# Weight splits through three buffers of 1024 columns instead of two of 1152

## The chip, the core and the metric

The kernel runs on one core of a Trainium2 chip. The metric is the device time of one execution in microseconds (us), and the median over several runs stands for a kernel. The engines have short names here: PE multiplies matrices (PEld is its loading of weights), DVE, ACT and POOL work element by element, SP only issues DMAs. Every engine works off its own queue in order.

## What is computed

A two-layer encoder on one sequence of 512 positions with 1024 channels. Each layer is a half-weighted FFN, four mixers side by side on slices of one input projection, and a second half-weighted FFN.

```python
D_MODEL, SEQ, DEPTH, D_FF = 1024, 512, 2, 2816
N_GROUPS = GROUP_HEADS = 4          # GROUP_WIDTH 256, HEAD_DIM 64

def swiglu(x, w_gate, w_up, w_down):
    return (jax.nn.silu(x @ w_gate) * (x @ w_up)) @ w_down
...
# per layer: x += 0.5 * ffn1(norm(x)); x += mixers(norm(x)) @ w_out; x += 0.5 * ffn2(norm(x))

# rwkv7_mixer: a state per head, forward and backward over the sequence
def step(S, inp):
    r_t, k_t, v_t, kk_t, a_t, w_t = inp
    sa = jnp.einsum('bhvk,bhk->bhv', S, -kk_t)
    S = (S * w_t[:, :, None, :] + sa[..., None] * (kk_t * a_t)[:, :, None, :]
         + v_t[..., None] * k_t[:, :, None, :])
    return S, jnp.einsum('bhvk,bhk->bhv', S, r_t)
...
# retention_mixer: scores with a decay, states before and after a chunk, a norm per head, a gate
# mla_mixer: latent queries and keys (ranks 384 and 128), softmax attention over all 512 positions
# short_conv_mixer: three taps, two gates
```

## The kernel before

All activations lie transposed, 128 channels on the partitions by 512 positions: `x[d]` for d in 0 to 7. A matmul in full precision is made of three in a fast format: `split` (L320) turns a raw weight tile into a rounded part `w_hi`, cast on ACT at L327, and a rest `w_lo`, subtracted on DVE at L328; `mm3` then issues hi·hi (L338), hi·lo (L339) and lo·hi (L340). Both parts come from rings of two buffers of 1152 columns of fp32. Raw weights come by DMA from SP into a ring of two buffers of 2048 columns (`load`).

The FFN (L344) goes over 11 of the 22 blocks of hidden channels at a time: a load of 2048 columns, split into 1024 for the gate (tile `pg`) and 1024 for the up projection (`pu`), 24 matmuls each; then eight output tiles `pd`, whose weights come in splits of 768 and 640 columns.

The mixers (`Mixers.run`) use `proj` for 128 columns of the input projection (tile `pj`, a split of 1024, done in pieces of 512), and `proj_nat` for two projections with positions on the partitions (tile `pn`, L502 to L504): `wrv` with 256 columns, the RWKV values, and `wtv` with 288, the retention's values and MLA's rotary key. `proj_nat` holds all weights of a projection at once, as two halves of four channel blocks each: 1024 columns for `wrv`, 1152 for `wtv`. `gd` and `ckv` are the weights projected after `wrv`, `tg` (two blocks, the retention's gate) those after `wtv`.

The RWKV state runs in eight chain steps. In each, on PE: scores `psG` L1059, values into `zy` L1078 and L1081, eight solves with the inverted blocks `NR` (L1090), the state (L1105) and eight outputs (L1123). Between them DVE and ACT copy: `Zs`, the solved values `ch` (DVE L1093 for one direction, ACT L1094 for the other), `Sd` and `Yn`. Beside the chain PE has matmuls of MLA (`m_pq`, the scores `m_sc` L781, the transposes of probabilities `m_ptp` L793) and of retention (`ret_ps`, `ret_po`, `ret_ss`, the broadcasts `ret_pb`). A softmax tile takes on DVE a maximum L783, a scaling of it L784, a reciprocal L787 and the scaling of the tile `m_p` L788, with an exponential on ACT (L786) between. Retention ends (`retention_end`) with a reciprocal root in many short steps (L235 to L241), copies `ret_sq` L253, products `ret_o` L671 and a split `ys` L513; the RWKV output is normed in L1155 to L1164. Then comes the output projection `po`.

The order in each queue is set when the program is built: a scheduler plays the instructions on a timeline of its own and takes, of those that are ready and whose buffers are free, the earliest in the code. Splits are moved ahead by 4000 places (`AHEAD`), and `in_turn` fixes the order within a group. So buffer counts set the order of instructions.

Tiles of the mixers and FFNs come from two pools: `vt`, NV = 19 tiles of 128x1024, and `ft`, NFS = 23 tiles of half that size.

Of the kernel before, what the change touches and what calls it, by code (L numbers as in the profile page):

```python
# [8 lines left out]
F32 = mybir.dt.float32  # L9
F32R = mybir.dt.float32r  # L10
# [5 lines left out]
P = 128  # L16
D = 1024
KD = D // P
# [116 lines left out]
class K:  # L135
# [3 lines left out]

    NV, NFS = 19, 23

    def __init__(self, ctx, tc, I, out, dbg=None):
        self.ctx, self.tc, self.nc, self.I, self.out = ctx, tc, tc.nc, I, out
# [83 lines left out]
    def rsqrt(self, out, ss, n, scale, eps, who="r", op=ALU.add):  # L229

        V = self.nc.vector
        v = self.tmp.tile([P, 16], F32, name="rq_v", tag="rq_v" + who)[:, :n]
        t = self.tmp.tile([P, 16], F32, name="rq_t", tag="rq_t" + who)[:, :n]
        r = self.tmp.tile([P, 16], F32, name="rq_r", tag="rq_r" + who)[:, :n]
        V.tensor_scalar(v, ss, scale, eps, ALU.mult, op)  # L235
        V.tensor_scalar(r.bitcast(I32), v.bitcast(I32), 1, None, ALU.logical_shift_right)
        V.tensor_scalar(r.bitcast(I32), r.bitcast(I32), -1.0, float(0x5f3759df), ALU.mult, ALU.add)
        for i in range(3):
            V.tensor_tensor(t, r, r, ALU.mult)
            V.scalar_tensor_tensor(t, t, -0.5, v, ALU.mult, ALU.mult)  # L240
            V.scalar_tensor_tensor(out if i == 2 else r, t, 1.5, r, ALU.add, ALU.mult)  # L241
# [77 lines left out]

    def split(self, raw, n, piece=1024):  # L320

        hi = self.ring.tile([P, 1152], F32R, name="w_hi", tag="w_hi", bufs=2)[:, :n]
        lo = self.ring.tile([P, 1152], F32R, name="w_lo", tag="w_lo", bufs=2)[:, :n]
        with self.tc.high_priority(offset=AHEAD):
            for a in range(0, n, piece):
                s = slice(a, min(a + piece, n))
                self.split_hi = self.nc.scalar.copy(hi[:, s], raw[:, s])  # L327
                self.nc.vector.tensor_tensor(lo[:, s], raw[:, s], hi[:, s].bitcast(F32), ALU.subtract)  # L328
        return hi, lo
# [83 lines left out]
class Mixers:  # L413
# [72 lines left out]
    def proj_nat(self, src, n, dst):  # L486

        k, l = self.k, self.l
        half = KD // 2 * n
        if 2 * half <= 2048:  # L490
            raw = k.load(src, 2 * half)
            pieces = [k.split(raw[:, half * o:half * o + half], half, 2 * n) for o in range(2)]
        else:
            pieces = [k.split(k.load(src[:, half * o:half * o + half], half), half, 2 * n) for o in range(2)]
        mm = self.nc.tensor.matmul
        for tt in range(NT):
            ps = k.ps("pn", "mm")[:, 0:n]
            sl = slice(P * tt, P * tt + P)
            for d in range(KD):
                hi, lo = pieces[d // 4]  # L500
                q = slice(n * (d % 4), n * (d % 4) + n)
                mm(ps, k.xh[d][:, sl], hi[:, q], start=d == 0, stop=False)  # L502
                mm(ps, k.xh[d][:, sl], lo[:, q], start=False, stop=False)
                mm(ps, k.xl[d][:, sl], hi[:, q], start=False, stop=d == KD - 1)  # L504
            a = 0
            for o, w in dst(tt):
                self.nc.vector.tensor_scalar(o, ps[:, a:a + w], self.rn[:, tt:tt + 1], None, ALU.mult)
                a += w
# [767 lines left out]
```

## Time and profile before

| | us |
|---|---|
| median of 3 runs | 2170.99 (2170.92 to 2171.12) |
| profiled execution, device time | 2169.86 |
| its span, first to last instruction | 2168.1 |
| PE busy | 2131.3 |
| DVE busy | 1113.3 |
| ACT busy | 711.6 |

PE's busy share is 98%. Layer 1's mixers run from about 392 to 740 us of the span, those of layer 2 from 1457 to 1808; the rest is FFNs, apart from the first 6 and the last 17 us. Back-to-back matmuls of 128x512 in the fast format start every 0.23 us; their records are longer and overlap.

### The profile page before, as it was taken

Reading aid. Unit: us, or ns where it says so; the run is one execution under the profiler, and the core shown is the slowest. Engines: PE = TensorE matmul, PEld = TensorE weight load, DVE = VectorE, ACT = ScalarE, POOL = GpSimd, SP = SyncE. Lnnn points to the kernel's source line nnn. Section 1 sums busy time; section 2 is a strip of 40 time slices with the busy share of each in tenths; the row PEclk is TensorE's granted clock in tenths of the full one; section 3 lists DMA queues with packets and bytes.
Section 4 is the critical chain, followed back from the end, with each engine's and each line's share of the span. In section 5 each row is a group of like instructions: output and inputs, shape, how many; then the busy total and the mean of one; then the engine's idle time right before and its main releaser. Section 6 shows DMA issues by size and latency. Waiting matters only on the chain.

```text
span 2168.1 us, 27576 instructions
## 1 busy us (share of the span) xinstructions
PE 2131.3 (98%) x11316; PEld 1714.9 (79%) x11316; DVE 1113.3 (51%) x1917; ACT 711.6 (33%) x1061; POOL 122.4 (6%) x146
## 2 busy tenths in 40 slices
PE   8999999999999999999999999999999999999997
PEld 7888888788666888888888888887886578888886
DVE  4454445676577543443544444457756865434433
ACT  4222223443233422222322222335323243222232
POOL 2000001000020100000100000010001210000001
PEclk9999999999999999999999999999999999999998
DMA  4223224144002322322322232242330122223222
GB/s 170 97 85 106 98 95 151 61 118 129 20 21 86 116 98 85 117 97 79 106 97 91 94 109 95 92 147 72 116 101 21 64 90 105 91 80 111 97 87 79
DMA packets 65294, 204.68 MB, mean 94 GB/s; under 512 B 26512, under 2 KB 26768, under 8 KB 50960
## 3 DMA queue, kind: packets, MB, share of 16 engines
q1 hardware_dynamic: 65168, 202.93, 28.5%
q8 instruction: 88, 1.44, 0.3%
q14 instruction: 38, 0.31, 0.0%
HBM read 191.37 MB, written 9.44 MB: 93 GB/s over the span
## 4 chain that ended last, share of the span: by engine, by line
PE 93%; DVE 4%; ACT 1%; DMA 1%; issue 1%; SPq 0%; DVEq 0%; ACTq 0%
PE pg L338 7%; PE pg L340 7%; PE pg L339 7%; PE pu L338 7%; PE pd L340 7%; PE pu L339 7%; PE pd L339 7%; PE pd L338 7%; PE pu L340 7%; PE pj L338 4%; PE pj L339 4%; PE pj L340 4%; PE po L338 1%; PE po L339 1%; PE po L340 1%; PE m_pq L758 1%
## 5 line engine op out<-in xcount | busy, mean ns | idle before, releaser
L327 ACT CAST w_hi<-w_raw 128x1024 fp32r<-128x1024 f32 (+4 forms) x446 | 367.4, 836 | 1132.1 <-PE pg L339 308.9
L328 DVE TENSOR_TENSOR w_lo<-w_raw,w_hi 128x1024 fp32r<-128x1024 f32 (+4 forms) x446 | 425.7, 962 | 229.4 <-ACT w_hi L327 220.1
L338 PE MATMUL pg<-xg,w_hi 128*128 128x512 f32 x704 | 275.5, 391 | 6.2 <-ACT w_hi L327 6.2
L340 PE MATMUL pg<-xg,w_lo 128*128 128x512 f32 x704 | 275.0, 391 | 0.0
L339 PE MATMUL pg<-xg,w_hi 128*128 128x512 f32 x704 | 274.9, 390 | 0.0
L338 PE MATMUL pu<-xg,w_hi 128*128 128x512 f32 x704 | 274.1, 389 | 0.4 <-ACT w_hi L327 0.4
L339 PE MATMUL pu<-xg,w_hi 128*128 128x512 f32 x704 | 274.2, 389 | 0.0
L340 PE MATMUL pu<-xg,w_lo 128*128 128x512 f32 x704 | 273.9, 389 | 0.0
L340 PE MATMUL pd<-g,w_lo 128*128 128x512 f32 x704 | 273.9, 389 | 0.0
L338 PE MATMUL pd<-g,w_hi 128*128 128x512 f32 x704 | 273.9, 389 | 0.0
L339 PE MATMUL pd<-g,w_hi 128*128 128x512 f32 x704 | 273.9, 389 | 0.0
L372 DVE TENSOR_TENSOR g<-pu,s 128x512 f32<-128x512 f32 x88 | 60.9, 692 | 274.0 <-PE pu L340 271.2
L369 DVE TENSOR_TENSOR s<-pg,rb 128x512 f32<-128x512 f32 x88 | 60.8, 691 | 206.5 <-PE pg L340 206.4
L338 PEld LDWEIGHTS pg<-xg,w_hi 128*128 128x128 f32 x704 | 132.7, 188 | 33.7 <-ACT w_hi L327 6.2
L340 PEld LDWEIGHTS pg<-xg,w_lo 128*128 128x128 f32 x704 | 132.7, 188 | 28.5 <-DVE w_lo L328 1.0
L339 PEld LDWEIGHTS pg<-xg,w_hi 128*128 128x128 f32 x704 | 132.7, 188 | 28.0 <-DVE xg L274 0.5
L338 PEld LDWEIGHTS pu<-xg,w_hi 128*128 128x128 f32 x704 | 132.2, 188 | 28.1 <-ACT w_hi L327 0.9
L340 PEld LDWEIGHTS pu<-xg,w_lo 128*128 128x128 f32 x704 | 132.2, 188 | 27.5 <-DVE w_lo L328 0.2
L339 PEld LDWEIGHTS pd<-g,w_hi 128*128 128x128 f32 x704 | 132.2, 188 | 27.5
L338 PEld LDWEIGHTS pd<-g,w_hi 128*128 128x128 f32 x704 | 132.2, 188 | 27.4
L340 PEld LDWEIGHTS pd<-g,w_lo 128*128 128x128 f32 x704 | 132.2, 188 | 27.4
L339 PEld LDWEIGHTS pu<-xg,w_hi 128*128 128x128 f32 x704 | 132.2, 188 | 27.3
(294 smaller groups left out, 2706.5 us busy)
## 6 DMA issues: line engine op xcount, KB each, us to landing
w_raw<-gu SPq DMA_DIRECT2D x87, 1024.0 KB, 4.8
w_raw<-dn SPq DMA_DIRECT2D x64, 704.0 KB, 4.2
w_raw<-win SPq DMA_DIRECT2D x22, 1024.0 KB, 5.1
w_raw<-wo SPq DMA_DIRECT2D x32, 256.0 KB, 2.8
xs<-x SPq DMA_DIRECT2D x16, 256.0 KB, 4.7
x<-xs SPq DMA_DIRECT2D x16, 256.0 KB, 5.7
w_raw<-wtv SPq DMA_DIRECT2D x4, 576.0 KB, 4.2
x<-xT SPq DMA_DIRECT2D x8, 256.0 KB, 5.9
```

Of the source, the lines that this page charges most:

```text
L327: self.split_hi = self.nc.scalar.copy(hi[:, s], raw[:, s])
L328: self.nc.vector.tensor_tensor(lo[:, s], raw[:, s], hi[:, s].bitcast(F32), ALU.subtract)
L338: T_.matmul(ps, hi, xh, start=start, stop=False)
L339: T_.matmul(ps, hi, xl, start=False, stop=False)
L340: T_.matmul(ps, lo, xh, start=False, stop=stop)
L369: V.tensor_tensor(s, pg, rb, ALU.mult)
L372: V.tensor_tensor(g, pu, s, ALU.mult)
L758: mm(pq, wq[i][:, P * h:P * h + P], qa[i], start=i == 0, stop=i == 2)
```

## The change

Both rings of split weights get three buffers of 1024 columns. `proj_nat` cuts the weights into pieces of as many channel blocks as go into 1024 columns: two of four for `wrv`, as before, and three (three, three and two blocks) for `wtv`; one load serves two pieces. `ft` has 21 tiles instead of 23, and one of the small tiles of the reciprocal root has one buffer instead of two.

```diff
-    NV, NFS = 19, 23
+    NV, NFS = 19, 21
...
-        v = self.tmp.tile([P, 16], F32, name="rq_v", tag="rq_v" + who)[:, :n]
+        v = self.tmp.tile([P, 16], F32, name="rq_v", tag="rq_v" + who, bufs=1)[:, :n]
...
-        hi = self.ring.tile([P, 1152], F32R, name="w_hi", tag="w_hi", bufs=2)[:, :n]
-        lo = self.ring.tile([P, 1152], F32R, name="w_lo", tag="w_lo", bufs=2)[:, :n]
+        hi = self.ring.tile([P, 1024], F32R, name="w_hi", tag="w_hi", bufs=3)[:, :n]
+        lo = self.ring.tile([P, 1024], F32R, name="w_lo", tag="w_lo", bufs=3)[:, :n]
...
-        half = KD // 2 * n
-        if 2 * half <= 2048:
-            raw = k.load(src, 2 * half)
-            pieces = [k.split(raw[:, half * o:half * o + half], half, 2 * n) for o in range(2)]
-        else:
-            pieces = [k.split(k.load(src[:, half * o:half * o + half], half), half, 2 * n) for o in range(2)]
+        per = 1024 // n
+        pieces = []
+        for a in range(0, KD, 2 * per):
+            b = min(a + 2 * per, KD)
+            raw = k.load(src[:, n * a:n * b], n * (b - a))
+            for c in range(a, b, per):
+                e = min(c + per, b)
+                pieces.append(k.split(raw[:, n * (c - a):n * (e - a)], n * (e - c), 2 * n))
...
-                hi, lo = pieces[d // 4]
-                q = slice(n * (d % 4), n * (d % 4) + n)
+                hi, lo = pieces[d // per]
+                q = slice(n * (d % per), n * (d % per) + n)
```

After the new lines in `proj_nat`, every line of the changed kernel has a number higher by 2 (L1123 is L1125 there). Three places show how the order of instructions moves.

On PE, the end of `wtv` in layer 1 and the beginning of `tg`, before:

```order
L504 MATMUL pn<-w_hi,xg_2499 128x288
L338 MATMUL pj<-xg_2130,w_hi 128x512
L339 MATMUL pj<-xg_2130,w_hi 128x512
L340 MATMUL pj<-xg_2130,w_lo 128x512
L338 MATMUL pj<-xg_2181,w_hi 128x512
L339 MATMUL pj<-xg_2181,w_hi 128x512
```

and in the changed kernel:

```order
L506 MATMUL pn<-w_hi,xg_2499 128x288
L338 MATMUL pj<-xg_2130,w_hi 128x512
L339 MATMUL pj<-xg_2130,w_hi 128x512
L338 MATMUL pj<-xg_2130,w_hi 128x512
L339 MATMUL pj<-xg_2130,w_hi 128x512
L340 MATMUL pj<-xg_2130,w_lo 128x512
```

The second L338 and L339 are those of the second block of `tg`, and stand ahead of the first L340 now. At `gd`, after `wrv`, it is the other way round: there the two of `ckv` stood ahead of the first L340 before, and no longer do.

On PE, the last chain step of layer 1, from its last solves to its outputs, before:

```order
L1090 MATMUL zy_3912<-ch_3910,NR_3049 64x64
L1090 MATMUL zy_3913<-ch_3911,NR_3050 64x64
L781 MATMUL m_sc<-m_kT,m_qT 128x512
L1123 MATMUL zy_3912<-ch_3910,Gm 64x64
L1123 MATMUL zy_3913<-ch_3911,Gm 64x64
```

and in the changed kernel:

```order
L783 MATMUL m_sc<-m_kT,m_qT 128x512
L1092 MATMUL zy_3912<-ch_3910,NR_3049 64x64
L1092 MATMUL zy_3913<-ch_3911,NR_3050 64x64
...
L1125 MATMUL zy_3912<-ch_3910,Gm 64x64
L1125 MATMUL zy_3913<-ch_3911,Gm 64x64
```

The outputs follow on the solves directly; the same holds for the first, the seventh and the eighth step of layer 2, and but for one matmul of 128x128 for the first step of layer 1 and the sixth of layer 2. Before, each step has an `m_sc` or at least five smaller matmuls there.

On DVE, behind the last chain step of layer 1, the rows that end with the fourth `m_p` after its copy `ch`, before:

```order
L240 SCALAR_TENSOR_TENSOR rq_t<-rq_t,rq_v 128x16
L788 TENSOR_SCALAR m_p<-m_p,sm 128x512
L1159 TENSOR_REDUCE gn_st<-gn_wk 128x8
L784 TENSOR_SCALAR sm<-sm,m_fqa 128x1
L241 SCALAR_TENSOR_TENSOR rq_r<-rq_t,rq_r 128x16
L787 RECIPROCAL sm<-sm 128x1
L783 TENSOR_REDUCE sm<-m_sc 128x1
L235 TENSOR_SCALAR rq_v<-gn_st 128x8
L239 TENSOR_TENSOR rq_t<-rq_r 128x16
L788 TENSOR_SCALAR m_p<-m_p,sm 128x512
```

and in the changed kernel:

```order
L790 TENSOR_SCALAR m_p<-m_p,sm 128x512
L789 RECIPROCAL sm<-sm 128x1
L673 TENSOR_TENSOR ret_o<-ret_o,ret_pb 128x512 x2
L1165 TENSOR_TENSOR gn_wk<-gn_wk,gn_wk_5088 128x512
L789 RECIPROCAL sm<-sm 128x1
L235 TENSOR_SCALAR rq_v<-gn_st 128x8
L785 TENSOR_REDUCE sm<-m_sc 128x1
L790 TENSOR_SCALAR m_p<-m_p,sm 128x512
L515 TENSOR_TENSOR ys_5188<-ret_o,ys_5188 128x512
L1166 TENSOR_TENSOR gn_wk<-gn_wk,gn 128x512
L515 TENSOR_TENSOR ys_5198<-ret_o,ys_5198 128x512
L790 TENSOR_SCALAR m_p<-m_p,sm 128x512
```

The products and splits that end retention (`ret_o`, `ys`) and, some rows further up, the two copies `ret_sq` stand ahead of the fourth `m_p` now; before they stood behind it. Layer 2 has the same.

## Rows read from the trace of the kernel before

**Rows 1.** The page's busy times: engine, us, share of the span, instructions.

```profile
PE 2131.3 (98%) x11316; PEld 1714.9 (79%) x11316; DVE 1113.3 (51%) x1917; ACT 711.6 (33%) x1061; POOL 122.4 (6%) x146
```

**Rows 2.** Windows: stretch, length, busy us of five engines, granted clock, DMA share, GB/s.

```profile
392.00:740.00 348.00, 339.16 (x2436) 255.48 (x2435) 238.18 (x537) 135.67 (x240) 36.79 (x49) 0.99 0.26 79
740.00:1457.00 717.00, 717.00 (x3185) 594.42 (x3184) 306.97 (x395) 210.68 (x276) 18.55 (x18) 1.00 0.30 99
1457.00:1808.00 351.00, 343.04 (x2460) 259.00 (x2459) 240.13 (x541) 136.47 (x242) 36.54 (x49) 1.00 0.26 82
```

**Rows 3.** PE's waits: what waited <- for what: us in total, times, longest.

```profile
PE pg L338 <- ACT w_hi L327: 6.2, 1, 6.2
PE m_sc L781 <- ACT m_p L786: 5.8, 4, 1.7
PE pj L340 <- DVE w_lo L328: 2.7, 2, 1.7
PE ret_po L646 <- DVE ret_ms L639: 2.1, 2, 1.1
PE zy L1105 <- DVE ch L1093: 1.5, 2, 0.7
PE zy L1078 <- ACT Yn L1132: 0.9, 2, 0.5
```

**Rows 4.** ACT's waits, the longest one.

```profile
ACT w_hi L327 <- PE pg L339: 308.9, 81, 5.6
```

**Rows 5.** PE's timeline at gd, layer 1: start, us, instruction, idle before.

```profile
428.33 0.50 PE L338 MATMUL pj<-xg,w_hi 128*128 128x512 f32 x1 [0.24 <-ACT w_hi L327]
```

**Rows 6.** DVE's timeline at gd, layer 1.

```profile
428.17 1.29 DVE L328 TENSOR_TENSOR w_lo<-w_raw,w_hi 128x512 fp32r<-128x512 f32 x2
```

**Rows 7.** PE's timeline at tg, layer 1.

```profile
475.90 0.50 PE L340 MATMUL pj<-xg,w_lo 128*128 128x512 f32 x1 [1.72 <-DVE w_lo L328]
```

**Rows 8.** DVE's timeline ahead of tg, layer 1.

```profile
474.29 0.69 DVE L567 TENSOR_TENSOR rsb<-rs,rb 128x512 f32<-128x512 f32 x1
474.89 0.35 DVE L972 TENSOR_TENSOR tmpR<-Nb,Rb 128x192 f32<-128x192 f32 x1
475.15 0.69 DVE L328 TENSOR_TENSOR w_lo<-w_raw,w_hi 128x512 fp32r<-128x512 f32 x1
```

**Rows 9.** PE's timeline in the fourth chain step (step 3 from 0), layer 1.

```profile
601.88 0.34 PE L1105 MATMUL zy<-ch 128*64 128x64 f32 x4 [0.73 <-DVE ch L1093]
```

**Rows 10.** PE's timeline at the end of the chain, layer 1.

```profile
653.21 0.68 PE L1090 MATMUL zy<-ch,NR 64*64 64x64 f32 x16
...
666.98 0.50 PE L338 MATMUL po<-ys,w_hi 128*128 128x512 f32 x1
```

**Rows 11.** DVE's timeline from the last copy of the chain on, layer 1.

```profile
654.14 0.40 DVE L1093 TENSOR_SCALAR ch<-zy 64x256 f32<-64x256 f32 x1
...
665.37 0.48 DVE L788 TENSOR_SCALAR m_p<-m_p,sm 128x512 f32<-128x512 f32 x1
...
670.76 0.76 DVE L253 COPY ret_sq<-r 128x512 f32<-128x512 f32 x2
...
672.11 0.68 DVE L671 TENSOR_TENSOR ret_o<-ret_o,ret_pb 128x512 f32<-128x512 f32 x1
672.71 0.16 DVE L239 TENSOR_TENSOR rq_t<-rq_r 128x8 f32<-128x8 f32 x1
672.78 0.68 DVE L671 TENSOR_TENSOR ret_o<-ret_o,ret_pb 128x512 f32<-128x512 f32 x1
...
674.34 0.68 DVE L513 TENSOR_TENSOR ys<-ret_o,ys 128x512 fp32r<-128x512 f32 x1
```

**Rows 12.** Windows after the inverse and at the end of the mixers, layer 1.

```profile
537.00:544.00 7.00, 7.00 (x21) 5.29 (x21) 0.27 (x1) 0.81 (x3) 2.76 (x5) 0.51 0.17 64
660.00:668.00 8.00, 5.09 (x16) 2.52 (x17) 8.00 (x30) 4.47 (x10) 1.27 (x1) 1.00 0.01 2
```

## What the change was predicted to do

> **What bounds the kernel now.** I read the busy times first: PE is busy 2131.3 us of a span of 2168.1 [rows 1], so about 37 us are all that shorter waits of PE can give; more only comes from the clock or from less work, and the change removes no matmul. Where the 37 us lie is read from the windows by stage [rows 2]: between the mixers PE is busy 717.00 of 717.00 us, so the FFNs have nothing to give. The mixers of layer 1 have 348.00 − 339.16 = 8.8 us of idle PE, those of layer 2 351.00 − 343.04 = 8.0 us. The rest is the start and the end of the program. The third view is PE's own waits [rows 3]. The longest, 6.2 us, is the first matmul of the program. Of the others, w_hi and w_lo account for little: pj L340 waits twice for w_lo, 2.7 us in all, and pj L338 0.5 us. The larger ones are in the chain of the RWKV state and in what follows it: m_sc L781 waits four times for the exponentials of the softmax (5.8 us), ret_po for its masked scores (2.1), zy L1105 for the solved values on DVE (1.5), zy L1078 for Yn (0.9).
>
> One view invites a wrong reading. ACT's cast w_hi L327 waits 308.9 us for pg's matmuls, and as much again for other tiles [rows 4]. That is a wait for a free buffer, and a third buffer removes much of it. But PE is not idle while ACT waits there, so this time is worth nothing.
>
> **The change part by part.** Three buffers in the FFN: the casts run one buffer further ahead. There is no PE wait to remove, so this is 0; below 0 is excluded by the windows.
>
> The natural projection wrv (256 columns) keeps two pieces, so the third buffer is free for the next weights, those of ckv, which are used next to gd's. Before, PE has gd's and ckv's first matmuls, then waits 0.24 us for ckv's w_hi [rows 5], because the cast waited for a buffer. That wait goes. But w_lo for gd stands on DVE right behind a long product that ends at 428.2, and takes until about 428.9 [rows 6]. PE, which now asks for it straight after gd's two first matmuls, waits for it instead of filling with ckv's: two matmuls of 0.23 (717.00 us / 3185, [rows 2]) fewer ahead of the wait. Price: +0.45 per layer, **+0.9** in all; ends 0 (DVE comes earlier) and +0.9.
>
> The projection wtv (288 columns) now takes three pieces, all three buffers, so nothing is loaded ahead during it; it has no wait of its own in the trace, and its matmuls stay as many. Behind it stands tg, where PE waits 1.72 us for w_lo [rows 7] and in layer 2 the rest of the 2.7 us, 1.0 [rows 3]. In the new order tg1's two first matmuls stand ahead of that wait (0.45 of cover), and one step of the inverse fewer, about 0.3, lies between the projection's last scaling and w_lo. But w_lo still stands behind rcb, rsb and a step of the inverse [rows 8]. I take −0.6 per layer, **−1.2**; ends −0.5 and −2.7 (all of it).
>
> Here the Trainium skill speaks for more: "Perfetto Trace Analysis", section "Optimizing Scalar/DVE Operations", says that where ScalarE or VectorE are not saturated but cause bubbles on other engines, breaking up instructions may let work end sooner. By that the whole 2.7 us would go and the sum below would be 1.5 us lower. The trace has DVE without a gap at that place [rows 8], so the condition does not hold there and I keep −1.2.
>
> With the projections over earlier against the chain, and with 21 tiles instead of 23, the scheduler moves retention and MLA about one chain step forward. This is the larger part. In each of the eight steps PE does eight solves (L1090), DVE copies the result (L1093), and the state and output matmuls need the copy. The solves of the last step end at 653.21 + 0.68 = 653.89, the copy at 654.14 + 0.40 = 654.54 [rows 10, 11]: 0.65 us in which PE needs other work. Before, each step has some there, the last one one m_sc. After, two steps of layer 1 and four of layer 2 have none or one small matmul of 0.1. Price: 6 × 0.65 − 0.2 = +3.7. In step 3 DVE was late in both layers (0.73 each, [rows 9]); in layer 1 that step now has about 2.6 us of cover, so 0.73 goes. Sum **+2.9**; ends +1 (the copy starts at once and the queue of PE is late anyway) and +6 (the copy is late by another 0.73 in some). The wait for Yn, 0.9 in two [rows 3], is covered in layer 1: **−0.5**. The wait of ret_po, 2.1 in two [rows 3], loses perhaps **−0.3** in layer 1.
>
> Last the end of the mixers. From the last copy on, DVE works without a gap, and PE follows it: it waits up to 1.7 us for the exponentials [rows 3] and comes to the output projection at 666.98 [rows 10]. The fourth scaling of a softmax tile (L788) after the copy starts at 665.37 [rows 11], 11.2 us after it; PE's last transposes before the output projection need it. In the new order the end of retention stands ahead of that fourth scaling, which it did not before: the two copies L253 (0.76 together), two products L671 and two L513. A step of 0.68 delays the next by 0.60 (672.11 to 672.71), a short one by 0.08 to 0.1 [rows 11]. Layer 1: 0.7 + 4 × 0.60, less one maximum (L783) of 0.6, plus eight short steps, 0.8: 3.3. Layer 2: 0.7 + 2.4, less two products of group norm, 1.2, plus eleven short steps, 1.1: 3.0. PE has no more work of its own ahead of it than before (eight small broadcasts more, four tiny sums fewer), so it waits as much longer: **+6.3**. Ends: 0, if PE had the time to fill, and +8, since in the new order eight more transposes, which need copies on ACT and DVE, stand ahead of the output projection.
>
> The two tiles fewer: no wait of PE in the trace is put down to such a tile, so I count 0; ends 0 and one wait like that of m_sc per layer, 1.7. The one buffer for rq_v: 0.
>
> Sum: 0.9 − 1.2 + 2.9 − 0.5 − 0.3 + 6.3 = **+8.1 us**. The profiled execution took 2169.86 us; with the sum 2178.0. The median of the runs is 1.1 above it, 2171.0, and I forecast the median: **2179.1**, 0.4% slower.
>
> **Rivals.** First, no change to speak of: in the mixers the queues sort themselves out, DVE catches up because the softmax of heads 2 and 3 and the retention have begun earlier, and the end costs 0 instead of 6.3. For it: DVE's work in the mixers is the same in sum, and only its order changed. Against: DVE shows no gap from the last copy to the end of the retention. Time: 2171.0 + 1.8 = 2172.8.
>
> Second, faster: the early retention and MLA pull the whole end of the mixers together. The place is the softmax; its mechanism is that m_sc finds its buffers free because the exponentials come before the retention's end reaches DVE. Then 5.8 of m_sc and 2.7 of w_lo go, the copies in the chain cost 2.9: 2171.0 − 5.6 = 2165.4. It decides as soon as the four softmax steps are queued some 3 us earlier against the last copy than before. Against: the order of DVE has them later, behind the retention's end.
>
> Third, the clock. PE had a granted clock of 0.51, so nearly all of it at the lower level of 1.2 GHz, in the 7 us after the many tiny matmuls of the inverse, 7 × 0.49 = 3.4 us lost, but 1.00 in the end of the mixers, 660 to 668, where it was busy only 5.09 of 8 us [rows 12]. So gaps of this size have not cost the clock here. The new waits there are longer, though, and a stretch at half speed would add 3.4 us in a layer, 2179.1 + 3.4 = 2182.5. "TensorE: Matmul & The Clock Gate", sections "HAM oscillation — how this bites in real kernels" and "Part 4: PE-mode transpose", in the Trainium skill, states that idle gaps bring PE back to half rate and that transposes do not count as busy in the same way; the end of the mixers has both, and by that rule this rival is the right one; the trace of before did not agree at that place.
>
> That the third buffer does nothing at all is the first rival with the sum at 0, 2171.0.
>
> **How the numbers follow.** Forecast 0.45; no change 0.28; faster 0.20; clock 0.07. By 0.2%, 4.3 us, about what a measurement can tell from no change, faster is below 2166.7, slower above 2175.3: faster 0.20, same 0.28, slower 0.52. The range reaches from the rival of faster, 2166, to the upper ends of the terms, some 7 us above the forecast, 2186.
>
> **What would show it.** In the new trace: PE's waits for w_lo at tg shorter than 1.7 and a new one at gd of some 0.5; zy L1107 and L1125 waiting for ch in six places; m_sc and m_ptp waiting 3 us longer per layer; the FFNs unchanged at 50 of 50 us. The forecast is wrong if the time between the last copy of the chain and the output projection is not longer than 12.8 us, or if the end is longer but PE's work there is less by as much.

## The result, and the profile after

The median of four executions each went from 2171.05 us to 2192.13 us: a ratio of 1.0096, 95% interval 1.0081 to 1.0111, so 21 us slower where 8 were forecast. The four executions of the changed kernel lie between 2189.5 and 2194.5.

The page's busy times of the changed kernel, span 2190.0 us, to be read against [rows 1]:

```profile
PE 2143.7 (98%) x11316; PEld 1724.8 (79%) x11316; DVE 1120.8 (51%) x1919; ACT 712.4 (33%) x1063; POOL 123.0 (6%) x146
```

The span is 21.9 us longer. PE is idle for 2190.0 − 2143.7 = 46.3 us instead of 36.8, 9.5 more. But PE is also busy 12.4 us longer, with the same 11316 matmuls. The second number is the larger, and no term of the forecast has it.

PE's waits after (columns as in [rows 3]):

```profile
PE m_sc L783 <- ACT m_p L788: 7.4, 8, 1.8
PE m_ptp L795 <- DVE m_p L790: 4.6, 3, 2.5
PE zy L1107 <- DVE ch L1095: 2.9, 3, 1.6
PE pj L340 <- DVE w_lo L328: 2.5, 2, 1.3
PE kk_ss L881 <- ACT kk_sq L878: 2.0, 2, 1.0
PE ret_po L648 <- DVE ret_ms L641: 1.6, 1, 1.6
PE zy L1125 <- DVE ch L1095: 1.6, 2, 1.1
PE zy L1080 <- DVE Sd L1117: 1.3, 2, 0.8
PE pn L504 <- DVE krn L509: 0.8, 1, 0.8
PE zy L1080 <- ACT Yn L1134: 0.5, 1, 0.5
```

The waits in the chain for `ch` and those at the end of the mixers for `m_p` have grown, as forecast; w_lo (`pj` L340) has hardly changed; `kk_ss` and the wait of `pn` for `krn` are new. To compare busy times, windows must hold the same matmuls, and those of [rows 2] begin and end inside a stage: the mixers' first projection starts at 370.73 and 1442.40 us of the kernel before. So here are windows from that projection to the first `pg` of the FFN behind it, and the FFNs in between (columns as in [rows 2]). Before:

```profile
370.73:720.39 349.66, 340.82 (x2448) 257.21 (x2446) 239.29 (x545) 135.33 (x244) 35.07 (x52) 0.99 0.26 80
720.39:1442.40 722.01, 722.01 (x3202) 598.20 (x3200) 309.40 (x392) 212.80 (x275) 20.26 (x15) 1.00 0.30 99
1442.40:1789.40 347.00, 339.04 (x2447) 256.14 (x2446) 238.68 (x544) 135.35 (x244) 34.82 (x52) 1.00 0.26 81
```

After:

```profile
370.40:725.59 355.19, 342.58 (x2448) 259.10 (x2446) 239.35 (x545) 135.28 (x244) 34.84 (x52) 0.98 0.26 79
725.59:1447.41 721.82, 721.82 (x3201) 598.18 (x3200) 311.85 (x393) 213.55 (x276) 20.26 (x15) 1.00 0.30 99
1447.41:1811.68 364.27, 350.26 (x2448) 264.14 (x2446) 240.46 (x544) 134.79 (x244) 34.98 (x52) 0.96 0.25 77
```

The FFNs between the mixers are unchanged. In the mixers PE is idle for 12.6 and 14.0 us, against 8.8 and 8.0, and it is busy 1.8 us longer in layer 1 and 11.2 in layer 2. So the added busy time is in the mixers, and most of it in those of layer 2. The granted clock, the third column from the right, is 0.98 and 0.96 there, against 0.99 and 1.00. Shorter windows show where the clock falls:

```profile
474.00:482.00 8.00, 6.66 (x21) 5.05 (x22) 7.57 (x17) 1.13 (x4) 0.00 (x0) 0.79 0.53 152
664.00:676.00 12.00, 7.22 (x24) 3.96 (x24) 11.76 (x40) 5.54 (x12) 0.00 (x0) 0.72 0.00 0
1490.00:1498.00 8.00, 7.04 (x47) 7.05 (x48) 5.70 (x20) 4.56 (x8) 0.00 (x0) 0.79 0.46 150
1638.00:1646.00 8.00, 7.54 (x50) 5.80 (x51) 5.10 (x20) 3.03 (x6) 0.80 (x2) 0.79 0.30 91
1726.00:1744.00 18.00, 15.73 (x130) 11.36 (x130) 12.64 (x38) 3.04 (x7) 3.86 (x3) 0.62 0.34 108
1754.00:1762.00 8.00, 6.17 (x19) 3.76 (x18) 6.94 (x23) 3.22 (x8) 0.00 (x0) 0.79 0.00 0
```

In the kernel before, the clock left full speed in two places between start and end, behind the inverse of each layer ([rows 12] has one). Here are six more. A granted clock between 0.5 and 1 over a window means that PE ran at 1.2 GHz for a part of it and at 2.4 GHz for the rest. In PE's timeline at `tg`, layer 1, this looks as follows (start, us, instruction):

```profile
476.04 0.63 PE L340 MATMUL pj<-xg,w_lo 128*128 128x512 f32 x1 [1.28 <-DVE w_lo L328]
476.47 0.63 PE L338 MATMUL pj<-xg,w_hi 128*128 128x512 f32 x1
```

One matmul of 128x512 starts every 0.43 us here, against 0.23 in the FFNs: nearly double the time for the same work, behind a wait of 1.28 us. The stretches that begin near 667, 1729 and 1756 us stand behind waits of 2.54, 1.60 and 1.83 us. The other two do not stand behind a wait of 1 us or more. Near 1640 us the waits just ahead are 0.81, 0.55 and 0.46 us, among small matmuls, and near 1493 us a wait of 0.99 us and sixteen matmuls of 128x2 come first:

```profile
1490.95 1.95 PE L881 MATMUL kk_ss<-con_t,kk_sq 128*128 128x2 f32 x16 [0.99 <-ACT kk_sq L878]
```

So this one trace leaves two readings: that waits bring the clock down, or that stretches of small matmuls do.

### The profile page after: what moved, and what is told of

The parts are those of the page before. It is cut to its first block, busy times and chain, and to the rows that moved or that the text cites. A ratio compares the mean times of both kernels' runs of the same rounds, so it can differ in the third digit from the quotient of the medians.

```text
span 2190.0 us, 27658 instructions
## 1 busy us (share of the span) xinstructions
PE 2143.7 (98%) x11316; PEld 1724.8 (79%) x11316; DVE 1120.8 (51%) x1919; ACT 712.4 (33%) x1063; POOL 123.0 (6%) x146
## 4 chain that ended last, share of the span: by engine, by line
PE 92%; DVE 4%; ACT 1%; DMA 1%; issue 1%; SPq 0%; DVEq 0%; ACTq 0%
PE pg L338 7%; PE pg L339 7%; PE pg L340 7%; PE pu L339 7%; PE pu L338 7%; PE pd L339 7%; PE pd L338 7%; PE pu L340 7%; PE pd L340 7%; PE pj L338 4%; PE pj L340 4%; PE pj L339 4%; PE po L339 1%; PE po L338 1%; PE po L340 1%; PE m_pq L760 1%
## 5 line engine op out<-in xcount | busy, mean ns | idle before, releaser
L327 ACT CAST w_hi<-w_raw 128x1024 fp32r<-128x1024 f32 (+5 forms) x448 | 368.1, 834 | 1109.0 <-PE pg L339 324.4
L328 DVE TENSOR_TENSOR w_lo<-w_raw,w_hi 128x1024 fp32r<-128x1024 f32 (+5 forms) x448 | 429.3, 965 | 205.2 <-ACT w_hi L327 195.8
L338 PE MATMUL pg<-xg,w_hi 128*128 128x512 f32 x704 | 275.5, 391 | 6.3 <-ACT w_hi L327 6.3
L339 PE MATMUL pg<-xg,w_hi 128*128 128x512 f32 x704 | 274.9, 391 | 0.0
L340 PE MATMUL pg<-xg,w_lo 128*128 128x512 f32 x704 | 274.9, 391 | 0.0
L339 PE MATMUL pu<-xg,w_hi 128*128 128x512 f32 x704 | 274.3, 390 | 0.0
L338 PE MATMUL pu<-xg,w_hi 128*128 128x512 f32 x704 | 274.1, 389 | 0.0
L340 PE MATMUL pu<-xg,w_lo 128*128 128x512 f32 x704 | 273.9, 389 | 0.0
L340 PE MATMUL pd<-g,w_lo 128*128 128x512 f32 x704 | 273.9, 389 | 0.0
L338 PE MATMUL pd<-g,w_hi 128*128 128x512 f32 x704 | 273.9, 389 | 0.0
L339 PE MATMUL pd<-g,w_hi 128*128 128x512 f32 x704 | 273.9, 389 | 0.0
L338 PEld LDWEIGHTS pg<-xg,w_hi 128*128 128x128 f32 x704 | 132.8, 189 | 33.9 <-ACT w_hi L327 6.3
L339 PEld LDWEIGHTS pg<-xg,w_hi 128*128 128x128 f32 x704 | 132.7, 189 | 28.0 <-DVE xg L274 0.7
L340 PEld LDWEIGHTS pg<-xg,w_lo 128*128 128x128 f32 x704 | 132.7, 188 | 27.8 <-DVE w_lo L328 0.3
L338 PEld LDWEIGHTS pu<-xg,w_hi 128*128 128x128 f32 x704 | 132.1, 188 | 27.9 <-ACT w_hi L327 0.4
L338 PEld LDWEIGHTS pd<-g,w_hi 128*128 128x128 f32 x704 | 132.1, 188 | 27.5
L340 PEld LDWEIGHTS pd<-g,w_lo 128*128 128x128 f32 x704 | 132.1, 188 | 27.5
L340 PEld LDWEIGHTS pu<-xg,w_lo 128*128 128x128 f32 x704 | 132.2, 188 | 27.3
L339 PEld LDWEIGHTS pd<-g,w_hi 128*128 128x128 f32 x704 | 132.1, 188 | 27.3
L339 PEld LDWEIGHTS pu<-xg,w_hi 128*128 128x128 f32 x704 | 132.1, 188 | 27.2
```

Of the source, the lines that this page charges most:

```text
L338: T_.matmul(ps, hi, xh, start=start, stop=False)
L339: T_.matmul(ps, hi, xl, start=False, stop=False)
L340: T_.matmul(ps, lo, xh, start=False, stop=stop)
```

## The experiments

The first theory was that the third buffer moves the order of the other matmuls, that this lengthens PE's waits, and that the waits bring the clock down, which costs as much again. Its rivals were that the fewer tiles or the pieces of `wtv` cost the time, and that the half-speed stretches have nothing to do with waits. All kernels but the second profile of the changed one were timed beside the kernel before.

| kernel | median us | ratio to before (95%) | span | PE busy | PE idle | clock |
|---|---|---|---|---|---|---|
| before | 2171.05 | 1 | 2168.1 | 2131.3 | 36.8 | 0.995 |
| after | 2192.13 | 1.0096 (1.0081 to 1.0111) | 2190.0 | 2143.7 | 46.3 | 0.987 |
| tiles21 | 2173.01 | 1.0011 (1.0001 to 1.0020) | 2170.9 | 2134.0 | 36.9 | 0.994 |
| solve_cover | 2190.88 | 1.0089 (1.0074 to 1.0104) | 2189.1 | 2149.7 | 39.4 | 0.987 |
| ret_last | 2181.43 | 1.0052 (1.0037 to 1.0067) | 2179.5 | 2136.9 | 42.6 | 0.992 |
| cover_and_last | 2188.58 | 1.0088 (1.0073 to 1.0103) | 2190.5 | 2146.9 | 43.6 | 0.988 |
| before_delay | 2186.61 | 1.0069 (1.0052 to 1.0086) | 2184.3 | 2137.7 | 46.6 | 0.989 |
| after_filled | 2187.88 | 1.0069 (1.0053 to 1.0085) | 2185.7 | 2148.3 | 37.4 | 0.991 |
| before_ret_last | 2177.80 | 1.0029 (1.0018 to 1.0040) | 2177.6 | 2135.0 | 42.6 | 0.994 |
| third_for_wtv | 2183.59 | 1.0059 (1.0044 to 1.0074) | 2183.6 | 2143.4 | 40.2 | 0.990 |
| third_for_ffn, then ffn_again | 2168.35, 2168.52 | 0.9990 (0.9981 to 1.0000), 0.9985 (0.9976 to 0.9994) | 2166.7 | 2134.1 | 32.6 | 0.995 |
| wtv_first_own | 2174.96 | 1.0013 (1.0005 to 1.0022) | 2173.9 | 2138.2 | 35.7 | 0.992 |

Span, busy and idle time (span less busy time) and clock are of one profiled execution of each; the ratio is to executions of the kernel before on the same chip, beside which each was timed.

**tiles21: only the tiles.**

```diff
-    NV, NFS = 19, 23
+    NV, NFS = 19, 21
```

> The kernel before with one edit: 21 half-size tiles instead of 23, rings of two buffers of 1152 as they were. Theory 1 (the third buffer moves the order, which lengthens PE's waits, and the waits bring the clock down): the order of the chain keeps its cover between solves and outputs here, so the time stays within 4 us of 2171. Rival (the two tiles fewer cause it): most of the 21 us appear here, 2185 to 2192.

2173.0 us: the two tiles fewer cost about 2 us (0.2 to 4.3 by the interval), so they are not the cause. PE's idle time is that of before (36.9 us), but it is made of other waits, to be read against [rows 3]:

```profile
PE pn L502 <- ACT w_hi L327: 5.2, 3, 4.2
PE po L338 <- ACT m_p L786: 2.7, 2, 1.4
PE m_sc L781 <- ACT m_p L786: 2.2, 4, 0.7
PE zy L1105 <- DVE ch L1093: 0.4, 2, 0.2
```

So the tiles alone do move the order. The waits for `ch` and those of the scores are shorter than before, and 4.2 us at once are spent on the cast of `wtv` in layer 2, where the kernel before had no wait.

**solve_cover: the chain's cover alone.** On the changed kernel:

```diff
-            self.in_turn([(solve, *x) for x in both])
+            solved = self.in_turn([(solve, *x) for x in both])
...
-                    for j in range(2):
-                        nc.tensor.transpose(pt[:, P * j:P * j + P], kb(d, j), ident)
+                    with self.tc.issue_after(solved.ins):
+                        for j in range(2):
+                            nc.tensor.transpose(pt[:, P * j:P * j + P], kb(d, j), ident)
```

> The changed kernel with one edit: in each chain step the transposes psT are pinned behind the last solve, so that PE has work there in steps 0 to 6, as before the change. Theory 1: the waits for ch shrink from 4.5 us to about 2, and the stretch at half speed behind them in layer 2 (1728 to 1743) goes; 2182 to 2187. Rival (the half-speed stretches have nothing to do with the waits in the chain): 2 to 3 us off, 2189 to 2190, and the mean clock stays at 0.987.

The waits behaved as the first theory has it, the time did not. The waits for `ch` on DVE fell from 4.5 to 2.0 us, and PE is idle 6.9 us less than after the change. But the time is only 1 us less, and PE is busy 6.0 us longer. This kernel has nearly the idle time of before (39.4 against 36.8) and nearly the time of after. What it lacks is the clock:

```profile
654.00:668.00 14.00, 12.35 (x74) 7.72 (x74) 13.26 (x39) 2.42 (x6) 5.56 (x5) 0.63 0.55 170
```

```profile
656.50 1.22 PE L1080 MATMUL zy<-Sd,KQ 128*128 128x128 f32 x4 [0.83 <-DVE Yn L1133]
```

So the time is not made by the sum of the waits: 2.6 us more of them went with 18.4 us more busy time. The rival's numbers (2189 to 2190, clock 0.987) came nearer than the theory's: shorter waits in the chain did not bring the clock back. In layer 1 it falls near 656.5 us, behind a wait of 0.83 us for Yn among small matmuls. What brings the clock down in the chain stays open.

**ret_last: the end of the mixers alone.** On the changed kernel:

```diff
-        self.retention_end()
         self.mla(1)
+        self.retention_end()
```

> The changed kernel with one edit: the end of the retention stands behind the softmax of heads 2 and 3 in the code, so DVE does the softmax first. Theory 1: the waits of m_sc and m_ptp in the end of the mixers fall from 12 us to some 7 in both layers together, and the half-speed stretches there (666 to 675, 1756 to 1760) go: 2182 to 2187. Rival (DVE has as much to do in either order, and PE waits for the retention instead): 2190 to 2194.

2181.4 us, 10.7 less than after, 0.6 below the expected range. PE's idle time fell by 3.7 us and its busy time by 6.8 (2.8 and 4.1 against the second profile of the changed kernel, below), and the clock stays at full speed between 650 and 690 us and from 1720 to the FFN. The order of DVE in the end of the mixers was worth about half of the loss, and of that half the clock was the larger part.

**cover_and_last: both.**

> The changed kernel with both edits, psT pinned behind the solves and the retention's end behind the softmax. Theory 1: PE's waits come back to near those of before, the clock to 0.993 or more, 2172 to 2179. Rival (the three buffers themselves cost, by more traffic of casts beside PE): not below 2185.

This failed. 2188.6 us, 7 more than with ret_last alone. The copies `Zs` in front of the solves come late here: PE waits 1.11 us for them in the last step of layer 1 and 1.55 in layer 2, 1.61 for Yn in each, and the clock is at half speed from 655 to 665 and from 1741 to 1747. That the pinned `psT` are the reason is not shown: the second profile of the changed kernel, without the pin, has such a wait of 1.45 us, too. The number is what the rival said, but its reason, casts that disturb PE, is not borne out by third_for_ffn below.

**before_delay: a delay on DVE, in the kernel before.** In `mla`, ahead of the scaled maximum of one softmax tile:

```diff
+                if h == 2 and qt == 2:
+                    late = V.tensor_scalar(dly, self.y[0][:, 0].bitcast(F32), sm[:, 0:1], None, ALU.mult)
+                    for _ in range(6):
+                        with self.tc.issue_after(late.ins):
+                            late = V.tensor_scalar(dly, self.y[0][:, 0].bitcast(F32), sm[:, 0:1], None, ALU.mult)
```

> The kernel before with seven idle products of 128x512 added on DVE in front of the third softmax tile of head 2, in each layer: 7 x 0.6 = 4.2 us that delay PE in the end of the mixers; the order elsewhere is as before. Theory 1 (a longer wait of PE brings its clock down for some us after it): PE's waits grow by 2 to 4 us in each layer, and a stretch at half speed appears behind them that was not there, 2 to 4 us of PE busy time more in each; 2179 to 2187, mean clock under 0.994. Rival (the clock does not follow such waits): the waits alone, 2175 to 2179, clock 0.995.

2186.6 us, 15.3 more than the kernel before. In the mixers of each layer the order up to the delay is that of the kernel before, but for a few matmuls in layer 2; behind it the order of DVE and PE differs as well. The added products took 0.47 us each instead of the 0.6 expected; DVE is busy 6.4 us longer, both layers together. PE's idle time grew by 9.8 us and its busy time by 6.4. The window of this kernel, and then the one of the kernel before for the same stretch:

```profile
662.00:678.00 16.00, 10.20 (x27) 5.67 (x28) 15.85 (x56) 5.81 (x13) 1.30 (x1) 0.57 0.00 1
```

```profile
662.00:678.00 16.00, 14.69 (x75) 8.99 (x74) 15.74 (x53) 7.67 (x17) 1.27 (x1) 1.00 0.00 1
```

PE's timeline of the delayed kernel, where the clock falls:

```profile
659.51 1.12 PE L782 MATMUL m_sc<-m_kT,m_qT 128*128 128x512 f32 x2
662.76 0.69 PE L802 MATMUL m_ptp<-con_t,m_p 128*128 128x128 f32 x2 [2.13 <-DVE m_p L797]
663.84 2.07 PE L782 MATMUL m_sc<-m_kT,m_qT 128*128 128x512 f32 x2 [0.39 <-ACT m_p L795]
670.56 2.07 PE L782 MATMUL m_sc<-m_kT,m_qT 128*128 128x512 f32 x2 [4.64 <-ACT m_p L795]
```

The clock is 0.57 over 16 us in one and 1.00 in the other. A score `m_sc` (two passes) takes 1.12 us ahead of the wait of 2.13 us and 2.07 behind it: the clock fell there, before the longest wait, 4.64 us. Layer 2 shows the same behind 2.12 us. So waits of a size that the changed kernel has, too (up to 2.54 us), can bring the clock down at the end of the mixers. The kernel before has waits of 1.68 and 1.24 us there, at a clock of 1.00:

```profile
661.59 1.13 PE L781 MATMUL m_sc<-m_kT,m_qT 128*128 128x512 f32 x2 [1.68 <-ACT m_p L786]
```

**after_filled: work in place of waits.** On the changed kernel, ahead of seven scores `m_sc` of heads 2 and 3, tied to their places:

```diff
+                        with self.tc.issue_after(warm.ins):
+                            for _ in range(4):
+                                warm = mm(wp, wy[:, 0:P], wy, start=True, stop=True)
```

> The changed kernel with 28 useless matmuls of 128x512 more in each layer, four ahead of each of seven scores m_sc of heads 2 and 3 (28 x 0.23 = 6.4 us of work per layer, 12.7 in all); the order up to the end of the mixers is that of the changed kernel. Theory 1 (PE's waits in the end of the mixers bring the clock down): the half-speed stretches there (666 to 675, 1756 to 1760) go, most of the added work fits into the waits, and in spite of it the time stays at 2188 to 2194. Rival (half-speed stretches come from something else, as transposes or many small matmuls): they stay, and the time grows to 2196 to 2204.

With 12.7 us of useless work more, by the estimate above, the kernel is not slower than after; by the medians it is 4.2 us faster (1.0069 against 1.0096). That it is faster at all is not clear of the spread: its executions took 2183.0 to 2189.5 us, those of after 2188.2 (after_again, on the same chip) to 2194.5. Windows of the end of the mixers:

```profile
655.00:664.00 9.00, 6.50 (x23) 4.80 (x23) 9.00 (x28) 1.87 (x3) 1.74 (x1) 0.81 0.14 51
664.00:676.00 12.00, 12.00 (x48) 8.14 (x47) 11.19 (x38) 6.52 (x15) 0.00 (x0) 1.00 0.00 0
1734.00:1746.00 12.00, 8.75 (x42) 6.24 (x43) 11.14 (x39) 2.90 (x6) 1.59 (x1) 0.72 0.25 89
```

Without the 12.7 us, PE is busy 2135.6 us, 8.1 less than after, and idle 37.4, 8.9 less. The stretch from 664 to 676, at 0.72 in both profiles of the changed kernel, has full speed; shorter ones at half speed stand behind the waits that were left ahead of the added work, 658 to 662 and 1736 to 1744. The median lies 0.1 us under the range of the theory and 8 under that of the rival.

**before_ret_last: the other order, in the kernel before.** The same two lines as in ret_last.

> The kernel before with the end of the retention behind the softmax of heads 2 and 3 in the code. Theory 1 (the order of DVE in the end of the mixers sets PE's waits there): there the softmax stood ahead already, so little changes, 2169 to 2173. Rival (the retention's end in front was better placed): 2174 to 2178.

2177.8 us, 6.5 more, so the rival holds: in the kernel before, the retention's end was well placed. The waits moved: those of the scores fell from 5.8 to 3.6 us, those of `m_ptp` grew from 0.2 to 4.3, and the output projection, which had none, waits 3.4 us. "Softmax first" is no rule.

**after_again: a second profile of the changed kernel.**

> The changed kernel once more, for a second profile. Theory 1: its waits are the same to 0.1 us; stretches at half speed lie behind the same waits in the chain and at its end, though not in every execution; the time is within 2189 to 2195. Rival (each stretch is bound to one instruction and comes always): all stretches are at the same places with the same length.

2188.2 us, 3.7 less than the first profiled execution and 0.8 under the expected range. Up to 1720 us the waits of 0.4 us and more are the same to 0.2 us. Behind that they are not. The first profile has this wait, which the second has not:

```profile
1727.04 0.65 PE L648 MATMUL ret_po<-ret_ms,ret_v 128*64 128x256 f32 x2 [1.60 <-DVE ret_ms L641]
```

The second waits 1.45 us in front of the last solves, the first does not. The clock of the second:

```profile
474.00:482.00 8.00, 6.43 (x31) 4.90 (x31) 7.90 (x20) 2.94 (x7) 0.00 (x0) 1.00 0.34 106
664.00:676.00 12.00, 7.19 (x21) 3.50 (x20) 11.90 (x36) 4.71 (x12) 0.15 (x1) 0.72 0.00 0
1726.00:1744.00 18.00, 14.32 (x146) 9.39 (x143) 15.67 (x47) 3.47 (x8) 4.51 (x4) 0.91 0.45 146
1754.00:1762.00 8.00, 8.00 (x39) 5.63 (x38) 7.85 (x28) 3.81 (x9) 0.00 (x0) 1.00 0.08 26
```

The wait of 1.28 us at `tg` is there in both; behind it the clock was 0.79 in the first and 1.00 in the second. Behind the last long wait for `m_p` in layer 2, 1.83 and 1.84 us, it was 0.79 and 1.00 (1754 to 1762). So the same wait in the same program does not always bring the clock down, and single executions of such a kernel differ by several us. The stretch from 664 to 676 is in both, at 0.72. From 1726 to 1744 the clock was 0.62 and 0.91, but there the waits differ. The rival, that each stretch is bound to one instruction and comes always, falls, and so does the theory that all waits are the same to 0.1 us.

**third_for_wtv and third_for_ffn: where the third buffer is used.** Both keep three pieces of `wtv` and 21 tiles. In the first the third buffer is a tile of its own for the third piece, and all other splits go over two buffers of 1024; in the second the FFNs' splits use it, too, every third one:

```diff
-    def split(self, raw, n, piece=1024):
+    def split(self, raw, n, piece=1024, own=False):
...
+        t, b = ("3", 1) if own else ("", 2)
+        hi = self.ring.tile([P, 1024], F32R, name="w_hi", tag="w_hi" + t, bufs=b)[:, :n]
+        lo = self.ring.tile([P, 1024], F32R, name="w_lo", tag="w_lo" + t, bufs=b)[:, :n]
```

> The changed kernel with the third buffer kept for the third piece of wtv alone: all other splits rotate over two buffers of 1024 columns; three pieces and 21 tiles as in the change. Theory 1 (the third buffer, used for all splits of the mixers, lets the projections run ahead and moves the other matmuls out of the chain's gaps): the chain has its cover again, PE's idle time in the mixers falls from 26 to about 17 us, 2171 to 2176. Rival (the three pieces of wtv or the 21 tiles are what costs): 2185 to 2192.

> As the last, and the FFNs' splits rotate over all three buffers, those of the mixers (but for wtv's third piece) over two. Theory 1 (in the FFNs PE never waits for a split, so the third buffer is worth nothing there): the same time as with the third buffer for wtv alone, within 3 us. Rival (running ahead in the FFNs pays at their ends): 3 to 5 us less.

third_for_ffn differs from the changed kernel only in that the mixers' splits other than `wtv`'s third piece use two buffers instead of three, and all of the loss is gone: 2168.4 us, and 2168.5 when it was timed again. That is 15 us less than third_for_wtv, where theory and rival had expected 5 at most. Its largest waits and the mixers' windows:

```profile
PE po L339 <- ACT m_p L791: 2.7, 2, 1.4
PE m_sc L786 <- ACT m_p L791: 2.2, 4, 0.7
PE pn L507 <- ACT w_hi L328: 2.1, 3, 1.2
PE zy L1110 <- DVE ch L1098: 0.4, 2, 0.2
```

```profile
392.00:740.00 348.00, 340.94 (x2439) 256.96 (x2438) 239.56 (x539) 137.05 (x242) 35.68 (x49) 0.99 0.26 79
1457.00:1808.00 351.00, 345.06 (x2462) 259.99 (x2461) 242.18 (x543) 138.72 (x245) 36.95 (x49) 1.00 0.26 82
```

The chain waits 0.4 us for `ch` (4.5 after), the end of the mixers about 5 for `m_p` (12 after), `tg` not at all for w_lo, and PE is idle 7.1 and 5.9 us in the mixers. third_for_wtv, in contrast, missed its range at 2183.6: of the 21 us, 12 are left. Its chain has cover again (0.2 us for `ch`), but `pn` waits 7.4 us for the casts of `wtv`, 4.6 of it at once in layer 2, and the clock is at half speed for about 7 us behind that and at two more places than before. Which rule of the scheduler lets a third buffer in the FFNs move the cast of `wtv` was not traced; tiles21 has such a wait (4.2 us) with two buffers throughout. PE's waits in the FFNs are the same in both to 0.5 us, so the FFNs gain next to nothing by themselves.

PE's idle time in the mixers is 13.0 us against 26.6 after, and the clock 0.995. Four kernels have 21 tiles and two buffers for the mixers' projections (tiles21, these two and wtv_first_own below): they wait 0.2 to 0.4 us for `ch` and 5.1 to 5.4 for `m_p`, the changed kernel 4.5 and 12.0. So these longer waits come from the third buffer as the mixers' projections use it, and not from the tiles or the three pieces. But the same four kernels lie between 2168 and 2184 us, with 2.1 to 7.4 us of waits for the casts at `pn`: the third buffer in the projections is not the only order that costs.

**ffn_again and wtv_first_own: is there more?** The first is third_for_ffn again, with more executions; the second gives the buffer of its own to the first piece of `wtv` instead of the third (`not pieces` in place of `len(pieces) == 2`, for `wtv` alone).

> Third buffer for the FFNs' splits and wtv's third piece alone, once more with more rounds, since it was close to the kernel before. Theory 1 (only PE's waits in the mixers and the clock behind them make a difference): PE's waits in the mixers are 12 us against 16 before, so 2 to 4 us less than before, 2167 to 2169. Rival (the difference was chance): within 1 us of before.

> As the last, but the buffer of its own goes to wtv's first piece instead of its third, so that its cast need not wait for the projection ahead. Theory 1: the wait of pn for w_hi at wtv (1.15 in layer 1) goes, the order of the chain stays, 2166 to 2169. Rival (the casts that move meet other work on ACT): 2169 to 2175 by a new wait or a half-speed stretch.

third_for_ffn stays 0.15% under the kernel before, interval 0.9976 to 0.9994, as its theory had it: 2.8 us less than the kernel before, and some 24 less than the changed one. wtv_first_own took 2175.0 us, the top of its rival's range and 6.4 more: the wait at `wtv` went in layer 1, but 2.56 us of it came in layer 2 and 1.79 us for w_lo at `tg` in layer 1, each with a stretch at half speed behind it.

The two profiles of third_for_ffn bear on the two readings of the clock. At `wrv` in layer 1 both have waits of 0.49 and 0.22 us, and then the sixteen matmuls of 128x2 without a wait. The same window, in third_for_ffn and then in ffn_again:

```profile
412.00:420.00 8.00, 7.29 (x47) 7.04 (x47) 4.70 (x15) 5.72 (x10) 0.00 (x0) 0.79 0.32 103
```

```profile
412.00:420.00 8.00, 7.29 (x59) 6.96 (x59) 6.01 (x20) 5.81 (x11) 0.00 (x0) 1.00 0.31 94
```

So the clock can fall behind small matmuls with no wait above 0.5 us, and it need not.

## Why the prediction was wrong

The sign was right, and so was the sum of the waits, nearly; the step that failed is the clock, which the sum put at nothing. Point by point:

| term | forecast, us | in the trace of after |
|---|---|---|
| `gd` and `wrv` | +0.9 | +0.1: no wait at `gd` (−0.5); at `wrv` 1.4 of `pn` went, 2.0 of `kk_ss` came |
| `wtv` and `tg` | −1.2 | +0.9: w_lo 2.7 to 2.5, new waits of 0.8 and 0.3 for `krn` |
| solved values `ch` | +2.9 | +3.0 (1.5 to 4.5) |
| Yn and Sd | −0.5 | +0.1 (Yn −0.4, Sd +0.5) |
| `ret_po` | −0.3 | −0.5 |
| end of the mixers, `m_p` | +6.3 | +6.0 (6.0 to 12.0) |
| idle time of PE in all | +8.1 | +9.5 |
| busy time of PE (clock) | 0 | +12.4 |

The two large terms came out nearly in sum, and by the steps that were given. In the end of the mixers of layer 1, DVE's rows of after, beside [rows 11], and PE's:

```profile
653.82 0.41 DVE L1095 TENSOR_SCALAR ch<-zy 64x256 f32<-64x256 f32 x1
...
668.52 0.47 DVE L790 TENSOR_SCALAR m_p<-m_p,sm 128x512 f32<-128x512 f32 x1
```

```profile
654.28 0.69 PE L1125 MATMUL zy<-ch,Gm 128*64 128x64 f32 x16 [1.08 <-DVE ch L1095]
...
666.84 0.44 PE L795 MATMUL m_ptp<-con_t,m_p 128*128 128x128 f32 x2 [2.54 <-DVE m_p L790]
669.04 0.69 PE L795 MATMUL m_ptp<-con_t,m_p 128*128 128x128 f32 x2 [1.76 <-DVE m_p L790]
```

The fourth scaling of `m_p` starts 14.7 us after the last copy; 11.2 + 3.3 = 14.5 was forecast. The last outputs wait 1.08 us for the copy rather than 0.65, since DVE had a maximum in front of it, but five places wait instead of six, and the sum is the same. That the waits for `m_p` grew by 6.0 us where 6.3 were forecast is in part luck: they grew by 4.0 in layer 1 and 2.0 in layer 2, against 3.3 and 3.0. The small terms failed: at `gd` w_lo came in time, and at `tg` the wait fell from 1.72 to 1.28 us in layer 1, as the two matmuls of cover give, but rose from 1.0 to 1.26 in layer 2, and waits for `krn` came in front. At `wrv` the prediction had left out PE's wait of 1.4 us at `pn`, which went, and the one of 2.0 at `kk_ss`, which came. Together the first two rows missed by 1.3 us.

The failed step is the clock: the sum takes PE's busy time as unchanged. The clock stands in the third rival alone, as another outcome beside the waits, with a chance of 0.07 and 3.4 us in one layer, because "gaps of this size have not cost the clock here". Measured were 12.4 us of busy time more for the same 11316 matmuls, most of them in the mixers of layer 2, with half-speed stretches at six more places. The reason given rested on one place in one execution: waits of 1.68 and 1.24 us at a clock of 1.00 [rows 12]. It was stretched to waits of 2.5 us, and to the chain with its many small matmuls, although the one stretch at half speed that the prediction shows stands behind the tiny matmuls of the inverse [rows 12]. And the size of a single wait does not tell: behind 1.72 us at `tg` [rows 7] the clock stayed at 1.00 in the kernel before, behind 1.28 us there it fell in one execution of the changed kernel and not in the other. Nor is the clock an alternative to longer waits: it came on top of them. The sign that was named for a wrong forecast, an end that is not longer than 12.8 us, could not catch this: in layer 1 the output projection starts 21.7 us after the last copy. Counting two stretches of 3.4 us a layer would give 2179.1 + 13.6 = 2192.7, but that count is read from the result, and layer 1 with its 1.8 us does not bear it out. What was known ahead allowed a range for the clock, not a number.

"TensorE: Matmul & The Clock Gate" in the Trainium skill, section "HAM oscillation — how this bites in real kernels", tells of a matmul kernel in which waits for DMA between bursts of matmuls bring PE back to half rate. Its waits are longer than the 2.5 us of the changed kernel; before_delay agrees, with 0.57 against 1.00 over the same 16 us, and has the fall behind a wait of 2.13 us.

For the end of the mixers the runs show that longer waits bring the clock down (before_delay, ret_last). For the chain, where the longest stretch lies (0.62 from 1726 to 1744), they do not: solve_cover took waits away there and the clock did not come back. Small matmuls may do there what longer waits do elsewhere, as at `wrv` in third_for_ffn; no run separates the two, and that part of the cause stays open.

The other rivals fell: the queues did not sort themselves out, and the softmax was not earlier. "Three buffers in the FFN: 0" was right for the FFNs themselves (721.82 us against 722.01); third_for_wtv and third_for_ffn show that the buffer there can still move the order in the mixers. "The two tiles fewer: 0" was near in time, about 2 us, but the tiles moved waits of 4 us. That the end costs because DVE does the retention first was shown by ret_last, for about half of the loss; that neither the tiles nor the pieces are behind it, by tiles21 and third_for_ffn.

## What to carry to other kernels

A deeper ring is not free even where it fits: it lets work run ahead, and a scheduler that fills gaps with that work can take it from the gaps that come later. Give the extra buffer only to the stage that is shown to wait for one, and compare the order in the others. On a kernel whose PE is the bound, give the clock a term of its own beside the new waits, and make it a range: against the kernel before, PE's busy time grew by 3.7 us with 5.8 of idle time in before_ret_last, by 12.4 with 9.5 in the changed kernel, and by 18.4 with 2.6 in solve_cover.

## What the runs showed of the hardware that was not expected

Useless matmuls can be free on an engine that is the bound: 12.7 us of them ahead of the waits at the end of the mixers did not make the kernel slower. The clock behind one and the same wait is not fixed: 0.79 and 1.00 behind the same 1.28 us in two executions. It can also fall with no wait above 0.5 us, behind sixteen matmuls of 128x2 (0.79 and 1.00 again in two executions of one kernel). The executions of the changed kernel spread over 5.0 us, and the differing clock can be one reason. In the Trainium skill, "TensorE: Matmul & The Clock Gate", section "What's actually happening", says that the gate's timing is not tied to the start of a kernel; the two profiles fit that. And idle time alone does not tell the clock: solve_cover had 2.6 us more of it than the kernel before, and 18.4 us more busy time.
